# A decoder layer in float32: attention's values as split products, and its stages ordered head by head

## The chip, the cores and the metric

The kernel runs on one core of a Trainium2 chip. The metric is the time of one execution on the device in microseconds (us). Three runs of the kernel before took 1278.5 to 1279.03 us, median 1278.52. An execution that was profiled took 1277.71 us.

## The reference

One layer with a sequence of 1024 rows and a width of 1024, all in float32. A convolution branch and an attention branch are computed from the same normalised input and merged. Only attention matters here. It has 24 heads of 64 columns in three groups of eight, with a window and a stride for each group:

```python
DILATION_GROUPS = ((128, 1), (512, 4), (2048, 16))
...
scores = jnp.einsum('bdhnqe,bdhnke->bdhnqk', qb, kb) * (e ** -0.5)
scores = jnp.where(mask, scores, NEG_INF)
m = jnp.max(scores, axis=-1)
p = jnp.exp(scores - m[..., None])
den = jnp.sum(p, axis=-1)
o = jnp.einsum('bdhnqk,bdhnke->bdhnqe', p, vb) / den[..., None]
...
m_all = jnp.maximum(jnp.maximum(maxes[0], maxes[1]), maxes[2])
wts = [d_g * jnp.exp(m_g - m_all) for m_g, d_g in zip(maxes, dens)]
att = (wts[0]*outs[0] + wts[1]*outs[1] + wts[2]*outs[2]) / (wts[0] + wts[1] + wts[2])
y_att = (att * silu(z_att)) @ w_att_out
```

Queries are taken in blocks of 128. A block sees its own block of keys and, in the first two groups, also the one before it where there is one; the third group's blocks are packed so that each sees 128 keys.

## The kernel before, in words

Large products are made of three float32r products each: a float32 operand is written as a high part (ScalarE copies it into float32r) and a low part (VectorE or GpSimd subtracts the high part), and high x high, high x low and low x high are added up in PSUM. `split` (line 51) makes the parts, `mm3` (line 69) the products. One such product has a stationary operand of 128 x 128, loaded by its own LDWEIGHTS, and 512 moving columns.

The stretch that the change touches is a loop over slots (line 980 and on). In each slot TensorE first does one half of a projection half: twelve products of 512 columns (`pieces`), for the weights of k and q of the next heads and, at the end, for the gates. Behind it stands attention for one stage. There are twelve pairs of heads (j, g), four j by three groups g, and eight stages to a pair: a stage is two query blocks of one head, and before the change the two heads alternate from stage to stage. In slot s TensorE does, in this order, the scores of stage s, the turn (transposes) of stage s-2 and the values of stage s-3. Only TensorE's order is written out by hand; the other engines' and SyncE's orders are set by a scheduler that works on the recorded program.

- *Scores* (lines 843, 844). The stationary operand is q with its high part twice, or q_low (`ql`), the moving one k with both parts stacked over partitions; 128 or 256 keys. VectorE adds the mask and takes the row maximum (847), multiplies the two maxima by -1/8 (`nm`, 850), ScalarE takes the exponential and the row sum (852).
- *Turn* (860). Each 128 x 128 block of probabilities is transposed into PSUM `t` and copied into SBUF as `pt`, by VectorE in even stages (865) and by ScalarE in odd ones (863).
- *Values* (875). For each block of keys one float32 product of `pt` (stationary) with 64 columns of `vt`, into PSUM `o`; ScalarE copies `o` out after four stages (878).
- *Parts and moves.* A projection of k and q for one pair comes in two units (`part` 0 carries the rotated columns, lines 709 to 712, `part` 1 the others). `Parts` writes high and low parts into `kqp` (720, 721), a buffer of which there are two, and SyncE moves them into the stacked tiles: k2 and q2 of both heads when a part is made (`move_kq`), q_low of both heads and both parts later, in stage 4 of the pair before (`load_low`, with v's load). k2, q2 and ql have two tiles each, used in turn by pairs.
- *Combination.* After the third group of a j, `combine` reads the three groups' results back, weighs them by their maxima and row sums (897 to 922) and turns them (926); it is fed into later slots step by step through `beside`.

LEAD is the number of slots before the first stage, 13.

## Time and profile before

| | before |
|---|---|
| median of three runs | 1278.52 us |
| the profiled execution | 1277.71 us |
| its span, first to last instruction | 1275.9 us |
| TensorE busy | 1248.6 us (98%) |
| VectorE busy | 890.5 us (70%) |
| ScalarE busy | 476.8 us (37%) |
| GpSimd busy | 94.7 us (7%) |

Matmul groups of the page overlap in time, since a product begins before the one ahead of it has ended. What one product costs is therefore read from the distance between starts in the order of time, and how full the engine is from its idle time. Attention runs from about 676 to 1095 us of the span.

### The profile page before, as it was taken

What the parts mean: (1) busy time and instruction counts of PE and PEld (TensorE: products, weight loads), DVE (VectorE), ACT (ScalarE), POOL (GpSimd) and SP (SyncE); (2) the same over time, 40 slices, a digit from 0 to 9 for tenths busy, and PEclk for the clock granted to TensorE, in tenths of its full rate; (3) what the DMA queues carried; (4) which work ended last, traced back from release to release, by engine and by line L of the source; (5) the groups of instructions that cost most, each with busy time, mean ns of one, the idle gap of its engine ahead of it and who ended that gap; (6) DMA issues with size and microseconds to landing.
All of it is one profiled execution on the core that took longest, in us unless ns stands there. A gap on an engine that the chain in (4) does not pass through costs nothing.

```text
span 1275.9 us, 16604 instructions
## 1 busy us (share of the span) xinstructions
PE 1248.6 (98%) x6148; PEld 1050.6 (82%) x6148; DVE 890.5 (70%) x1576; ACT 476.8 (37%) x911; POOL 94.7 (7%) x78
## 2 busy tenths in 40 slices
PE   6999999999999999999999999999999989999997
PEld 4777888888888888888888888888888878888886
DVE  6777999999999986853345546766766563349544
ACT  4653212111222246720015545545444467534211
POOL 0000000000000000000042111111101012100000
PEclk9999999999999999999999999999999999999999
DMA  9522311211211112545666456576575566659221
GB/s 366 186 95 68 114 60 53 102 50 50 91 58 50 50 52 89 167 164 198 149 171 152 120 130 162 135 198 149 140 206 137 147 166 190 205 176 316 98 100 67
DMA packets 85526, 171.53 MB, mean 134 GB/s; under 512 B 11203, under 2 KB 41027, under 8 KB 85445
## 3 DMA queue, kind: packets, MB, share of 16 engines
q1 hardware_dynamic: 69024, 157.66, 41.9%
q10 hardware_dynamic: 16420, 12.80, 3.3%
q8 instruction: 49, 0.80, 0.3%
q14 instruction: 33, 0.26, 0.1%
HBM read 105.74 MB, written 33.23 MB: 109 GB/s over the span
## 4 chain that ended last, share of the span: by engine, by line
PE 91%; DVE 4%; DMA 2%; ACT 2%; issue 1%; SPq 0%; ACTq 0%; DVEq 0%
PE d L73 22%; PE d L75 22%; PE d L74 22%; PE o L875 4%; PE d L1070 2%; PE d L1069 2%; PE d L467 2%; PE d L466 2%; PE d L1071 2%; PE d L465 2%; PE t L860 2%; PE s L844 1%; PE s L843 1%; PE d L249 1%; PE d L247 1%; PE d L248 1%
## 5 line engine op out<-in xcount | busy, mean ns | idle before, releaser
L73 PE MATMUL d<-hh,whi 128*128 128x512 f32 x1072 | 427.5, 399 | 1.5 <-DVE gs L632 0.9
L74 PE MATMUL d<-hl,whi 128*128 128x512 f32 x1072 | 417.6, 390 | 1.9 <-DVE hl L347 1.9
L75 PE MATMUL d<-hh,wlo 128*128 128x512 f32 x1072 | 418.5, 390 | 0.0
L406 DVE SCALAR_TENSOR_TENSOR v<-u,cw,v 128x1024 f32<-128x1024 f32 x232 | 280.5, 1279 | 0.0
L75 PEld LDWEIGHTS d<-hh,wlo 128*128 128x128 f32 x1072 | 201.2, 188 | 43.9 <-POOL wlo L58 0.7
L74 PEld LDWEIGHTS d<-hl,whi 128*128 128x128 f32 x1072 | 201.7, 188 | 41.7 <-DVE hl L347 2.8
L73 PEld LDWEIGHTS d<-hh,whi 128*128 128x128 f32 x1072 | 201.6, 188 | 40.9 <-ACT whi L57 1.3
L57 ACT ACTIVATE whi<-wraw 128x512 fp32r<-128x512 f32 (+1 forms) x107 | 88.0, 834 | 269.6 <-PE d L74 236.1
L58 POOL TENSOR_TENSOR wlo<-wraw,whi 128x512 fp32r<-128x512 f32 (+1 forms) x56 | 84.8, 1529 | 658.0 <-ACT whi L57 556.2
L852 ACT ACTIVATE sb<-sb,nm 128x128 f32<-128x128 f32 (+1 forms) x192 | 85.0, 444 | 86.9 <-DVE nm L850 82.6
L847 DVE CUSTOM_DVE_ANT_0 sb<-s,mask 128x128 f32<-128x128 f32 (+1 forms) x192 | 59.7, 347 | 61.6 <-PE s L844 54.8
L875 PE MATMUL o<-vt,pt 128*128 128x64 f32 x560 | 73.5, 267 | 1.1 <-ACT pt L863 0.5
L875 PEld LDWEIGHTS o<-vt,pt 128*128 128x128 f32 x560 | 70.1, 192 | 2.1 <-DVE pt L865 1.3
L58 DVE TENSOR_TENSOR wlo<-wraw,whi 128x1024 fp32r<-128x1024 f32 (+1 forms) x51 | 57.9, 1137 | 15.6 <-ACT whi L57 15.0
L844 PE MATMUL s<-k,ql 128*128 128x128 f32 (+1 forms) x192 | 51.0, 279 | 3.2 <-DMA ql<-kqp 3.2
L465 PE MATMUL d<-vh,hh 128*128 128x512 f32 x128 | 49.8, 389 | 0.0
L466 PE MATMUL d<-vl,hh 128*128 128x512 f32 x128 | 49.8, 389 | 0.0
L467 PE MATMUL d<-vh,hl 128*128 128x512 f32 x128 | 49.8, 389 | 0.0
L73 PE MATMUL d<-uh,whi 128*128 128x512 f32 x128 | 49.8, 389 | 0.0
L74 PE MATMUL d<-ul,whi 128*128 128x512 f32 x128 | 49.8, 389 | 0.0
L75 PE MATMUL d<-uh,wlo 128*128 128x512 f32 x128 | 49.8, 389 | 0.0
L632 DVE TENSOR_TENSOR gs<-d,sgc 128x512 f32<-128x512 f32 x16 | 11.1, 691 | 54.9 <-PE d L75 48.8
(224 smaller groups left out, 1758.5 us busy)
## 6 DMA issues: line engine op xcount, KB each, us to landing
wraw<-in_w_t SPq DMA_DIRECT2D x67, 512.0 KB, 4.3
k<-kqp SPq DMA_DIRECT2D x96, 128.0 KB, 2.6
q<-kqp SPq DMA_DIRECT2D x96, 128.0 KB, 2.4
wa<-in_w_ada SPq DMA_DIRECT2D x16, 512.0 KB, 5.9
rd<-oscr SPq DMA_DIRECT2D x8, 792.0 KB, 5.1
ql<-kqp SPq DMA_DIRECT2D x48, 128.0 KB, 2.4
wraw<-in_w_v SPq DMA_DIRECT2D x11, 512.0 KB, 3.6
x<-in_xT SPq DMA_DIRECT2D x8, 512.0 KB, 10.2
```

Source lines behind the costliest of these rows:

```text
L57: nc.scalar.activation(hi, raw, AF.Copy)
L58: (lo_eng or nc.vector).tensor_sub(lo, raw, hi.bitcast(F32))
L73: nc.tensor.matmul(ps, lh, rh, start=start, stop=False)
L74: nc.tensor.matmul(ps, lh, rl, start=False, stop=False)
L75: nc.tensor.matmul(ps, ll, rh, start=False, stop=stop)
L406: nc.vector.scalar_tensor_tensor(d, u[:, k:k + S], cw[:, ct, k:k + 1], d, op0=mult, op1=add)
L465: nc.tensor.matmul(ps, hh[:, k, ts_], rh, start=k == 0, stop=False)
L466: nc.tensor.matmul(ps, hh[:, k, ts_], rl, start=False, stop=False)
L467: nc.tensor.matmul(ps, hl[:, k, ts_], rh, start=False, stop=k == KT - 1)
L844: nc.tensor.matmul(ps[:, c:c + w], self.ql[:, h, ts_], self.k2[:, h, ks], start=False, stop=True)
L852: nc.scalar.activation(sb[:, c:c + w], sb[:, c:c + w], AF.Exp, bias=nm[:, t - tp:t - tp + 1], scale=SCALE, accum_out=ov[:, t, h, 64:65])
L875: nc.tensor.matmul(self.po[:, t % 4, h], pt[:, c + i:c + i + P], self.vt[:, kb, r], start=i == 0, stop=i + P == w)
```

## The change

The values' product becomes float32r. The turned probabilities are split into `ph` and `pl`, each stage by ScalarE and VectorE together, and v is split too: a tile of one head holds for each block of 128 keys 64 columns of the high part and, side by side, 64 of the low part. Each block of keys then has two products, `ph` and `pl` as stationary operands with the same 128 moving columns, and all four products of parts are computed. PSUM `o` holds one head's results in two halves, which VectorE adds into `ov` after two stages (line 889).

To have tiles for this, k, q and q_low become tiles of one head, three each, used in turn by heads, and the eight stages of a pair go head by head: four stages of the first, four of the second. The moves go head by head as well: those of the first head when a part is made, those of the second one slot later or, for part 0, four slots before the pair begins, each with its q_low. v is loaded five slots ahead into a raw tile and split in steps. The mask pass multiplies by -1/8 and takes the minimum, so that its result serves as the exponential's bias and `nm` goes. LEAD becomes 11.

```diff
-    def pair_tile(n, name, dt=F32R):
-        return stk.tile([P, 2, S], dt, name=name, tag=f"s{n}")
+    def head_tile(tag, name):
+        return stk.tile([P, S], F32R, name=name, tag=tag)
...
     def move_kq(n, part, h):
+        i = turn_of(n, h)
         if not part:
-            k2[n], q2[n] = pair_tile(n % 2, "k2"), pair_tile(2 + n % 2, "q2")
-        move(k2[n], 0, n, part, 0, 0)
-        move(k2[n], 64, n, part, 0, 1)
-        move(q2[n], 0, n, part, 1, 0)
-        move(q2[n], 64, n, part, 1, 0)
+            k2[n, h], q2[n, h] = head_tile(f"k{i}", "k2"), head_tile(f"q{i}", "q2")
+        move(k2[n, h], 0, n, part, 0, 0, h)
+        move(k2[n, h], 64, n, part, 0, 1, h)
+        move(q2[n, h], 0, n, part, 1, 0, h)
+        move(q2[n, h], 64, n, part, 1, 0, h)
+        move(q_low[i], 0, n, part, 1, 1, h)
...
+        for h in range(2):
+            v = v2[n, h] = stk.tile([P, 8, P], F32R, name="vt", tag=f"v{turn_of(n, h)}")
+            src = raw[:, :, 64 * h:64 * h + 64]
+            nc.scalar.activation(v[:, :, 0:64], src, AF.Copy)
+            nc.vector.tensor_sub(v[:, :, 64:128], src, v[:, :, 0:64].bitcast(F32))
             yield
...
-            tp, h, o, out_ = st_ // 2 * 2, st_ % 2, 0, []
+            tp, h, o, out_ = st_ % 4 * 2, st_ // 4, 0, []
...
-                    out=sb[:, c:c + w], in0=ps[:, c:c + w], in1=mk, scale=1.0, scalar=-3e38, op0=add, op1=mx,
+                    out=sb[:, c:c + w], in0=ps[:, c:c + w], in1=mk, scale=-SCALE, scalar=3e38, op0=add, op1=ALU.min,
                     accum_out=ov[:, t, h, 65:66])
-            nc.vector.tensor_scalar(nm, ov[:, tp:tp + 2, h, 65], -SCALE, None, op0=mult)
             for t, c, w in spans:
-                nc.scalar.activation(sb[:, c:c + w], sb[:, c:c + w], AF.Exp, bias=nm[:, t - tp:t - tp + 1],
-                                     scale=SCALE, accum_out=ov[:, t, h, 64:65])
+                nc.scalar.activation(sb[:, c:c + w], sb[:, c:c + w], AF.Exp, bias=ov[:, t, h, 65:66],
+                                     scale=-1.0, accum_out=ov[:, t, h, 64:65])
...
-            pt = self.pt[st_] = ap_.tile([P, 512], F32, name="pt", tag="pt", bufs=2)
-            if st_ % 2:
-                nc.scalar.activation(pt[:, :o], ps[:, :o], AF.Copy)
-            else:
-                nc.vector.tensor_copy(pt[:, :o], ps[:, :o])
+            hi, lo = self.pt[st_] = [ap_.tile([P, 512], F32R, name=x, tag=x, bufs=2) for x in ("ph", "pl")]
+            split(hi[:, :o], lo[:, :o], ps[:, :o])
...
-                    nc.tensor.matmul(self.po[:, t % 4, h], pt[:, c + i:c + i + P], self.vt[:, kb, r],
-                                     start=i == 0, stop=i + P == w)
-            if st_ % 4 == 3:
-                nc.scalar.activation(self.ov[:, tp - 2:tp + 2, :, 0:64], self.po, AF.Copy)
+                    for x in range(2):
+                        nc.tensor.matmul(self.po[:, t % 4], parts[x][:, c + i:c + i + P], v[:, kb],
+                                         start=i == 0 and x == 0, stop=i + P == w and x == 1)
+            if st_ % 2:
+                nc.vector.tensor_reduce(self.ov[:, tp - 2:tp + 2, h, 0:64],
+                                        self.po.rearrange("p t (x c) -> p t c x", x=2),
+                                        axis=mybir.AxisListType.X, op=add)
...
-    LEAD, TURN, VAL = 13, 2, 3
+    LEAD, TURN, VAL = 11, 2, 3
...
+            for n, part in due:
+                move_kq(n, part, 0)
+                in_steps(moves(n, part, 1), [slot_ if n == 0 else slot_ + 1 if part else 8 * n - 4])
+            n = (slot_ + 5) // 8
+            if slot_ == v_slots(n)[0] and 0 <= n < len(order):
+                in_steps(load_v(n), v_slots(n))
```

After attention the freed tiles serve for the merged heads and the output weights under other names.

Three places show how instructions moved. The first is TensorE's order in one slot of the first group, from the last scores on (`s` scores, `t` turned probabilities, `o` results, `d` a projection); equal instructions that follow each other are merged into one row. Before:

```order
L843 MATMUL s<-k_6631,q_6632 128x256
L844 MATMUL s<-k_6631,ql 128x256
L860 MATMUL t<-ident,sb 128x128 x3
L875 MATMUL o<-vt,pt 128x64 x3
L73 MATMUL d<-hh,whi 128x512
L74 MATMUL d<-hl,whi 128x512
```

The same place afterwards:

```order
L857 MATMUL s<-k_6886,q_6887 128x256
L858 MATMUL s<-k_6886,ql 128x256
L873 MATMUL t<-ident,sb 128x128 x3
L886 MATMUL o<-vt,ph 128x128
L886 MATMUL o<-vt,pl 128x128
```

Each block of keys has two instructions of 128 columns in place of one of 64, each with its own stationary operand; such pairs follow each other for all blocks of the stage, and the projection comes behind them as before.

The second is VectorE's order where the last but one combination begins (`rd` the results read back, `ma`, `w`, `wd` the weights, `sb,ov` a mask pass). Before:

```order
L850 TENSOR_SCALAR nm<-ov 128x2
L897 TENSOR_TENSOR ma<-rd 128x8
L898 TENSOR_TENSOR ma<-ma,rd 128x8
L902 TENSOR_TENSOR w<-rd,ma 128x8 x3
L908 TENSOR_TENSOR wd<-w,rd 128x8 x3
L909 TENSOR_TENSOR wd<-wd 128x8
L910 TENSOR_TENSOR wd<-wd 128x8
L911 RECIPROCAL wd<-wd 128x8
L913 TENSOR_TENSOR w<-w,wd 128x8 x3
L917 TENSOR_TENSOR rd<-rd,w 128x4x2x64 x2
```

Afterwards, from the first low part of probabilities behind that combination's small operations and its three products on:

```order
L58 TENSOR_TENSOR pl<-t,ph 128x384
L721 TENSOR_TENSOR rot<-d,ctab 128x512
L889 TENSOR_REDUCE ov<-o 128x4x64
L722 TENSOR_TENSOR sh<-sh,stab 128x512
L933 TENSOR_TENSOR rd<-rd 128x4x2x64
L723 TENSOR_TENSOR rot<-rot,sh 128x512
L935 TENSOR_TENSOR pr<-rd 128x512
L861 ISA sb,ov<-s,mask 128x256
L861 ISA ov 128x1
L732 TENSOR_TENSOR kqp<-rot,kqp 128x32x16
```

Behind these rows stand one more mask pass and the next low part, `pl`. The rotation of the next heads (721 to 723, 732), the sum of halves (889) and the combination (933, 935) now lie between two low parts; the small operations, three products, a shuffle and two mask passes lie between the first of the two and the one ahead of it.

The third is SyncE's queue for the last pair of heads. Before:

```order
L785 DMA k_8055<-kqp 32x1024 x4
L785 DMA q_8056<-kqp 32x1024 x4
L929 DMA atscr_95<-at 128x512
L785 DMA ql<-kqp 32x1024 x4
L675 DMA vt<-vscr 64x8x128 x2
```

Afterwards, the end of the second head's moves for part 0, and then the moves for part 1 of both:

```order
L794 DMA q_8655<-kqp 32x1024 x2
L794 DMA ql<-kqp 32x1024
L794 DMA k_8481<-kqp 32x1024 x2
L794 DMA q_8482<-kqp 32x1024 x2
L794 DMA ql<-kqp 32x1024
L918 DMA at<-zascr_91 128x512
L794 DMA k_8654<-kqp 32x1024 x2
L794 DMA q_8655<-kqp 32x1024 x2
L794 DMA ql<-kqp 32x1024
```

q_low's moves stand behind those of the same head's k and q, one for each head and part, and v's load stands further ahead.

## Rows read from the trace of the kernel before

**Rows 1.** The page: busy us, share of span, instructions; out<-in xcount | busy, mean ns.

```profile
PE 1248.6 (98%) x6148; PEld 1050.6 (82%) x6148; DVE 890.5 (70%) x1576; ACT 476.8 (37%) x911; POOL 94.7 (7%) x78
...
L875 PEld LDWEIGHTS o<-vt,pt 128*128 128x128 f32 x560 | 70.1, 192 | 2.1 <-DVE pt L865 1.3
```

**Rows 2.** Sums over 676 to 1095 us: PE, PEld, DVE, ACT, POOL busy; granted clock.

```profile
676.00:1095.00 419.00, 414.12 (x2439) 362.26 (x2438) 247.85 (x808) 219.09 (x577) 65.49 (x44) 1.00 0.60 156
```

**Rows 3.** TensorE in order of time: start us, length us, operation, xcount.

```profile
801.03 0.60 PE L860 MATMUL t<-ident,sb 128*128 128x128 f32 x4
801.46 1.00 PE L875 MATMUL o<-vt,pt 128*128 128x64 f32 x8
...
802.59 0.39 PE L74 MATMUL d<-hl,whi 128*128 128x512 f32 x1
802.82 0.40 PE L75 MATMUL d<-hh,wlo 128*128 128x512 f32 x1
...
805.46 0.28 PE L844 MATMUL s<-k,ql 128*128 128x256 f32 x1
805.58 0.60 PE L860 MATMUL t<-ident,sb 128*128 128x128 f32 x4
```

**Rows 4.** TensorE in order of time, scores of 128 keys.

```profile
862.01 0.22 PE L843 MATMUL s<-k,q 128*128 128x128 f32 x1
862.07 0.28 PE L844 MATMUL s<-k,ql 128*128 128x128 f32 x1
862.18 0.27 PE L843 MATMUL s<-k,q 128*128 128x128 f32 x1
```

**Rows 5.** TensorE in order of time, instructions that waited [idle us <-releaser].

```profile
776.69 0.50 PE L73 MATMUL d<-hh,whi 128*128 128x512 f32 x1 [0.19 <-DVE rot L710]
...
845.42 0.30 PE L844 MATMUL s<-k,ql 128*128 128x128 f32 x1 [0.29 <-DMA ql<-kqp]
...
1028.47 0.88 PE L875 MATMUL o<-vt,pt 128*128 128x64 f32 x6 [0.53 <-DVE pt L865]
...
1052.50 0.30 PE L844 MATMUL s<-k,ql 128*128 128x128 f32 x1 [2.87 <-DMA ql<-kqp]
...
1062.52 0.88 PE L875 MATMUL o<-vt,pt 128*128 128x64 f32 x6 [0.54 <-ACT pt L863]
```

**Rows 6.** VectorE's groups, 640 to 1100 us, by shape: busy us, mean ns | idle.

```profile
L847 DVE CUSTOM_DVE_ANT_0 sb<-s,mask 128x256 f32<-128x256 f32 x88 | 35.1, 419 | 21.4 <-PE s L844 21.4
L850 DVE TENSOR_SCALAR nm<-ov 128x2 f32<-128x2 f32 x96 | 27.9, 291 | 1.6
...
L721 DVE TENSOR_TENSOR kqp<-rot,kqp 128x512 fp32r<-128x512 f32 x24 | 23.8, 993 | 24.5 <-ACT kqp L720 22.8 <-DMA vt<-vscr 1.6
...
L710 DVE TENSOR_TENSOR rot<-d,ctab 128x512 f32<-128x512 f32 x24 | 16.4, 684 | 0.4
...
L813 DVE TENSOR_TENSOR vt<-vt,row 128x512 f32<-128x512 f32 x8 | 5.3, 692 | 0.1
```

**Rows 7.** The same for all widths of VectorE's copies.

```profile
L865 DVE COPY pt<-t 128x384 f32<-128x384 f32 (+2 forms) x48 | 26.0, 541 | 0.0
```

**Rows 8.** ScalarE's groups, 640 to 1100 us.

```profile
L863 ACT ACTIVATE pt<-t 128x384 f32<-128x384 f32 (+2 forms) x48 | 22.8, 476 | 38.3 <-PE t L860 38.3
...
L878 ACT ACTIVATE ov<-o 128x512 f32<-128x512 f32 x24 | 14.2, 592 | 7.9 <-PE o L875 7.8
```

**Rows 9.** VectorE in order of time at the last but one combination.

```profile
1020.83 0.34 DVE L908 TENSOR_TENSOR wd<-w,rd 128x8 f32<-128x8 f32 x3 [0.53 <-ACT w L903]
...
1021.76 2.55 DVE L913 TENSOR_TENSOR w<-w,wd 128x8 f32<-128x8 f32 x3
1024.23 1.88 DVE L917 TENSOR_TENSOR rd<-rd,w 128x512 f32<-128x512 f32 x3
```

**Rows 10.** SyncE's queue in order of time: the last moves of q_low.

```profile
1047.29 3.99 SPq L785 DMA_DIRECT2D ql<-kqp  x4
```

**Rows 11.** SyncE's waits: us in total, times, longest us.

```profile
SPq L785 <- DMA ascr<-gs: 11.6, 2, 6.1
```

More of the change, by code (lines that the diff above doesn't have):

```diff
@@ L773, in pieces @@
                 yield lambda half=half, s=s, ps=ps: consume(half, s, ps)
-    LOW, UP = slice(0, 64), slice(64, 128)
-    q_low = [pair_tile(4 + i, "ql") for i in range(2)]
-    for ql in q_low:
-        nc.gpsimd.memset(ql[UP].bitcast(F32), 0.0)
     k2, q2, v2 = {}, {}, {}
-    def move(dst, row, n, part, i, which):
-        for h in range(2):
-            src = parts_of[n, part][64 * i + 32 * h:64 * i + 32 * h + 32, which]
-            nc.sync.dma_start(dst[row + 32 * part:row + 32 * part + 32, h].bitcast(F32), src.bitcast(F32))
@@ L787, in move_kq, with turn_of @@
-    def move_kq(n, part):
-        if not part:
-            k2[n], q2[n] = pair_tile(n % 2, "k2"), pair_tile(2 + n % 2, "q2")
-        move(k2[n], 0, n, part, 0, 0)
-        move(k2[n], 64, n, part, 0, 1)
-        move(q2[n], 0, n, part, 1, 0)
-        move(q2[n], 64, n, part, 1, 0)
-    late = []
-    def load_low(n):
-        for part in range(2):
-            move(q_low[n % 2], 0, n, part, 1, 1)
-        v2[n] = stk.tile([P, 8, P], F32, name="vt", tag="vt", bufs=2)
-        v_load(v2[n], order[n][1], order[n][0])
-        if order[n][1] == 0:
+    def turn_of(n, h):
+        return (2 * n + h) % 3
@@ new lines, in move, with move_kq @@
+    def move(dst, row, n, part, i, which, h):
+        src = parts_of[n, part][64 * i + 32 * h:64 * i + 32 * h + 32, which]
+        nc.sync.dma_start(dst[row + 32 * part:row + 32 * part + 32].bitcast(F32), src.bitcast(F32))
+    def move_kq(n, part, h):
+        i = turn_of(n, h)
+        if not part:
+            k2[n, h], q2[n, h] = head_tile(f"k{i}", "k2"), head_tile(f"q{i}", "q2")
[4 more added lines that the diff above has]
+        move(q_low[i], 0, n, part, 1, 1, h)
@@ L821, in __init__ @@
             self.j, self.g = order[n]
-            self.ql = q_low[n % 2]
-            self.k2, self.q2, self.vt = k2.pop(n), q2.pop(n), v2.pop(n)
+            self.n = n
+            self.ql = [q_low[turn_of(n, h)] for h in range(2)]
             self.ov = ap_.tile([P, 8, 2, 66], F32, name="ov", tag="ov", bufs=2)
@@ L948, in w_out @@
             hi, lo = (pool.tile([P, 1024], F32R, name=f"{x}{n}{kp}") for x in ("oh", "ol"))
-        elif kp < 2:
-            if not pairs:
-                pairs.update({i: pair_tile(4 + i, "oh") for i in range(2)})
-            hi, lo = pairs[0][:, kp], pairs[1][:, kp]
-        elif n:
-            both = pair_tile(0, "o13")
+        elif n == 0 and kp > 1:
+            both = parts_tile("oh")
             hi, lo = both[:, 0], both[:, 1]
         else:
-            hi, lo = (stk.tile([P, 1024], F32R, name=x, tag="vt", bufs=2) for x in ("oh", "ol"))
+            hi, lo = (head_tile(x, "oh") for x in {(0, 0): ("l2", "v0"), (0, 1): ("v1", "v2"), (1, 3): ("k0", "k1")}[n, kp])
         split(hi, lo, raw)
@@ L968, in layer, with in_steps, moves, v_slots @@
     beside, heads = {}, {}
+    def in_steps(it, slots):
+        for x in slots:
+            beside.setdefault(x, []).append(it)
+    def moves(n, part, h):
+        move_kq(n, part, h)
+        yield
+    def v_slots(n):
+        return [8 * n + x for x in (-5, -3, -2, 0, 1)]
     with tc.manual_schedule(engines={nc.tensor.engine}):
@@ L981, in layer @@
                     heads[n] = Attend(n)
-                if st_ == 4 and n + 1 < len(order):
-                    load_low(n + 1)
                 heads[n].scores(st_)
@@ L1000, in layer @@
                 next(c)
-            for c in late:
-                for x in (2, 2, 3):
-                    beside.setdefault(slot_ + x, []).append(c)
-            late[:] = []
             j = slot_ - stages - VAL
```

65 lines of the change are left out of this document (38 added, 27 removed).

## The prediction

> **What bounds the kernel now.** I read the page's busy times first: TensorE 98% of the span [rows 1]. A share near one can still hide waiting, so the second view is the sum over the attention stretch, 676 to 1095 us, the only one whose code changes: TensorE 414.12 of 419 us, VectorE 247.85 (59%), ScalarE 219.09 (52%), granted clock 1.00, the 2.4 GHz level [rows 2]. The reader should see that TensorE's own instructions set the length here. All its idle time in the stretch is some 5 us; no other saving can be larger unless TensorE's instructions themselves get cheaper.
>
> Third, the order of time on TensorE, for what one instruction costs. The groups of the page overlap, so I take the distance between starts. In a slot with four key blocks the eight records of the value product begin at 801.46, and the second wide product behind them at 802.59; one wide product is 0.23 us apart from the next (802.59 to 802.82). So the eight took 1.13 - 0.23 = 0.90 us, 0.1125 us each [rows 3]. They are float32: the code's loops make 280 products, but the page counts 560 weight loads [rows 1] (and as many records), two for each. A float32r product with 128 moving columns stands in the score products: 862.01, 862.07, 862.18: 0.06 behind the first of a burst, then 0.11 us [rows 4].
>
> Fourth, TensorE's waits of the stretch, of which there are few: 2.87 and 0.29 us for q_low's move, 0.53 for VectorE's copy of the turned probabilities, 0.54 for ScalarE's, and three times about 0.19 for the rotation that frees a projection bank (one shown) [rows 5]. Together 4.8 us.
>
> **The change part by part.**
>
> *Value products.* 280 float32 products of 64 columns go, 560 float32r products of 128 columns come. Before: 560 x 0.1125 = 63.0 us. After: 560 x 0.11 = 61.6 to 62.7 us (0.11 to 0.112, the score products' distance). Change on the path: 0 to -1.4 us; I take -0.4. The reason for equality is that records of 64 columns, of 128 columns and of two kinds of number all stand 0.11 us apart, and what they share is one weight load of 128 columns each; the number of weight loads stays 560. The ends: nothing in this trace has a float32r product of 128 columns behind another at less than 0.11 except the first of a burst (862.01 to 862.07, 0.06 us [rows 4]), whose load lay under a wide product; at that price the 560 would save 29 us. Upwards, the 256-column products stand 0.12 us apart (805.46 to the turn's 805.58 [rows 3]), +4 us.
>
> A page of the Trainium skill speaks for a gain here: "TensorE: Matmul & The Clock Gate", section "Back-to-back issue gap", gives about 81 ns for each product of 128 columns in a sustained stream with its weight loads. By that the 560 would take 45 us and the sum would fall by 18 us. The score products at 110 ns do not bear it out for these types.
>
> *VectorE.* Removed: 96 negated maxima, 27.9 us (mean 291 ns, some stretched), and 48 copies of turned probabilities, 26.0 us. Added: 96 low parts. They have the same widths as the copies, twice as many, and a product read from PSUM beside SBUF costs what a copy of the same width does (684 ns for 512 columns; the copies' mean is 541 over 256 to 512), so 52.0 us. 48 sums of the two halves of a result, 512 elements read: no such operation is in the trace; between 0.42 us (a mask pass over 256 columns) and 1.0 us (the strided low part of k and q), that is 20 to 48 us, and I take 0.68, the two-source pass over PSUM of the same width: 33 us. 24 low parts of v at 0.69 (the row addition of the same width): 16.6 us. Sum 52.0 + 33 + 16.6 - 27.9 - 26.0 = +48 us (+35 to +63) [rows 6, 7]. VectorE goes from 59% to about 71% of the stretch. This lies beside TensorE as long as the low part of the probabilities is ready one slot later.
>
> *ScalarE.* 48 more high parts, +22.8 us; 24 copies of results go, -14.2; 24 high parts of v come at about the same 0.59, +14.2 [rows 8]. 52% becomes 58%, hidden.
>
> *The added wait.* TensorE's value product of a stage now waits for ScalarE's copy and then VectorE's subtraction, where before it waited for one of them. A slot lasts 4.55 us (801.03 to 805.58 [rows 3]); the turn ends it, so 4.55 - 0.59 (ScalarE's copy of 512 columns [rows 8]) - 0.69 (subtraction) = 3.3 us of slack remain. Queued behind a late subtraction on VectorE are the next stage's mask passes, the rotation that frees a projection bank, and the sums. The tight place is the combination of three groups, which now stands in VectorE's order beside the rotation of the next heads. By that order, between two subtractions: 14 small operations (1.6 us at 0.34 for three), a wait of 0.53 for ScalarE's weights, three products 1.88, the shuffle taken at 0.69, two mask passes 0.84, the subtraction of 384 columns 0.54: 6.1 us; then eight operations of 512 columns at 0.69 and two passes 0.84: 6.4 us. 12.5 us in two slots of 4.55 leaves VectorE 3.4 us late against 3.3 of slack: 0.1 us of waiting. Stretched operations come on top; three small products at this place once took 2.55 instead of 0.34 us [rows 6, 7, 9]. So 0.1 to 2.4 us at each of three such places; I take 1.0, that is +3.0, less the 0.53 that stands there already: +2.5.
>
> *Moves.* The 240 transfers of k, q and q_low stay 240, but q_low's now go with the same part's k and q. Before, both parts' stood last in SyncE's queue; the last four were begun at 1047.29, after SyncE had waited up to 6.1 us for a store of gates, and TensorE waited for them until 1052.50 [rows 5, 10, 11]. Afterwards q_low's first part goes out four slots earlier, and the moves of the last heads stand in the queue ahead of the first store of gates, which ScalarE issues only after them. Both waits for q_low go: -3.2 us. What could be late next is the new wait of the second head's moves for the scores three heads earlier; they are issued one slot after those end and used eight slots later, so I cost it at 0; if SyncE is held by it for more than two slots (9 us), the overwriting of the parts' buffer waits. The float32r parts of v are made three slots ahead, 0 as well.
>
> *Earlier start and shape.* LEAD 13 to 11 moves no TensorE instruction out of the loop. The rotation meets the long slots instead of the short ones, which gives its bank release half a microsecond more: -0.3 of the 0.6. Two fewer slots of exponentials share ScalarE with the gates' sigmoids: no TensorE wait is charged to that, 0.
>
> Sum against the profiled execution's own 1277.71 us (span 1275.9 and 1.8 around it): -0.4 + 2.5 - 3.2 - 0.3 = -1.4, so 1276.3. That execution lies 0.8 us under the median 1278.52, so in medians 1277.1 us.
>
> **Rivals.**
>
> *The waits go and none comes (faster).* -0.4 - 4.8 = -5.2: 1273.3 us. For it: VectorE has 12 percentage points less than a full load even so, and it loses the negated maxima, which ScalarE waited for. Against: the combination overfills two slots by the count above.
>
> *VectorE is late (slower).* One mechanism: the low part of the probabilities, at the three combinations. It decides once VectorE is more than 3.3 us behind. With sums at 1.0 us and one stretched group each, a combination costs 0.1 + 2.2 + 4 x 0.31 = 3.5 us and the lateness lasts into the next rotation with as much again less the slack regained, say 3.5 to 7 us a place; -3.6 - 0.3 - 0.5 + 3 x 4 to 3 x 5 = +7.6 to 10.6, about 1287 us. For it: VectorE had a wait there already at less load, [rows 5]. Against: 71% mean load.
>
> *The values get cheaper (faster).* If float32r products stood as the first of a burst does, 0.06 us apart, the 560 would take 34 us instead of 63: 29 us less, 1249 us. For it: that one distance. Against: every other distance in [rows 3, 4]. By the Trainium skill's 81 ns ("TensorE: Matmul & The Clock Gate", "Back-to-back issue gap") it would be an estimated 1260.
>
> **How the numbers follow.** My forecast, a shift of 1 to 2 us: 0.40. Waits gone: 0.29. Values cheaper: 0.03. VectorE late: 0.28. What a measurement of this kernel can tell from no change is about 0.2%, 2.6 us: below 1276.0 is faster, above 1281.1 slower. The forecast's own range is 1275 to 1280; 0.04 of its 0.40 lies below that bound and 0.01 above. Of the waits that go, 0.25 of 0.29 is faster; of VectorE late, 0.26 of 0.28 is slower. Faster 0.32, same 0.41, slower 0.27. The range of eight in ten reaches to most of both neighbours: 1272.0 to 1285.5.
>
> **What would show it.** Right: 560 records of the value product still about 0.11 us apart, with 560 weight loads; TensorE's wait for q_low gone; new waits, if any, named "pl" and lying at the three combinations; VectorE near 295 us in the stretch. Wrong: value records at 0.06 to 0.08 (the values step); waits for "pl" spread over all slots, or for "k2" and "q2" (the slack and the moves); a sum of halves over 1 us (VectorE's step).

## The result, and the profile after

The changed kernel took 1282.91 us (median of 8 runs, 1281.95 to 1284.77) against 1278.93 for the kernel before (8 runs, 1276.84 to 1280.48): ratio 1.0032, 95% interval 1.0021 to 1.0043, slower by 0.32%. The forecast was 1277.1, a fall of 1.4 us; the medians rose by 4.0. The profiled execution took 1283.09 us and its span is 1281.3, 5.4 us more than before. That is 1.4 us more than the medians differ, mostly because the profiled execution of the kernel before (1277.71) lies 1.2 us under its median. What follows accounts for the two profiled executions.

The page after, groups as in [rows 1, 6 and 8] (out<-in xcount | busy, mean ns | idle), and behind it the sums over the stretch of [rows 2]:

```profile
PE 1250.6 (98%) x6148; PEld 1050.8 (82%) x6148; DVE 932.8 (73%) x1600; ACT 489.6 (38%) x957; POOL 91.8 (7%) x79
...
L58 DVE TENSOR_TENSOR pl<-t,ph 128x384 fp32r<-128x384 f32 (+2 forms) x96 | 52.2, 544 | 29.1 <-ACT ph L57 28.4
...
L57 ACT ACTIVATE ph<-t 128x384 fp32r<-128x384 f32 (+2 forms) x96 | 46.0, 480 | 58.8 <-PE t L873 56.5
L886 PEld LDWEIGHTS o<-vt,pl 128*128 128x128 f32 x280 | 53.7, 192 | 4.5 <-DVE pl L58 4.4
L886 PEld LDWEIGHTS o<-vt,ph 128*128 128x128 f32 x280 | 53.5, 191 | 2.9 <-ACT ph L57 2.8
```

```profile
676.00:1095.00 419.00, 412.34 (x2420) 359.97 (x2419) 284.91 (x830) 230.70 (x620) 60.59 (x43) 1.00 0.59 158
```

TensorE's weight loads for the values are 560 as before and its instruction count is the same. In the stretch VectorE carries 37 us more, ScalarE 12. TensorE's waits after (us in total, times, longest):

```profile
PE o L886 <- DVE pl L58: 2.6, 9, 0.6
PE s L857 <- DVE ov L861: 2.3, 1, 2.3
...
PE o L886 <- ACT ph L57: 1.2, 2, 0.9
PE d L73 <- ACT gs L740: 0.9, 1, 0.9
```

No wait for q_low or for the rotation's bank is left [rows 5]; four others have come. Where they stand is best seen in the distance from the first scores of a slot to those of the next, taken from TensorE's order of time. "Free" is the changed kernel with its order mended (a_best4 below), in whose stages TensorE waits nowhere: what the slots take without a wait. Slots that a wait made longer are bold in the column after, and in the column before in the last row alone.

| slots, us | before | after | free |
|---|---|---|---|
| 0 to 3 (start) | 3.19 3.19 3.57 4.23 | 3.19 **5.73** 3.71 4.32 | 3.19 3.22 3.57 4.35 |
| 32 to 35 (first combination) | 4.55 4.56 4.45 4.84 | **4.97** 4.52 **5.37** **5.03** | 4.57 4.52 4.43 4.19 |
| 80 to 83 (third combination) | 4.55 4.56 4.45 5.41 | **4.97** 4.52 **5.85** 4.61 | 4.57 4.52 4.43 4.19 |
| 88 to 94 (last pair) | **7.61** 4.17 **5.05** 3.83 3.84 3.83 3.84 | 4.59 **5.01** 4.07 **4.41** 3.81 **5.38** 3.81 | 4.15 4.15 4.07 3.86 3.81 3.86 3.81 |

Before and after, 0.4 us of slots 35, 83 and 88 are the transposes of a combination, which are work; in the free version they stand in other slots. From first to last scores the free version takes 397.7 us, and the kernel before without its waits 397.8 (b_ql below, its one slot with a wait counted as 4.57). After takes 408.7: 2.6 of waiting at the start, 5.4 at the three combinations (1.8 each), 2.9 in the last pair; another 1.05 stands behind the last stage. Before took 405.0: 3.5 for q_low, 1.2 for the rotation's bank, 1.4 at the combinations, 1.0 in the last pair. The difference of the waits, 12.0 - 7.1 = +4.9 us, is the 5.4 us between the spans but for 0.5 us. These waits are what the slots lost, which is more than the idle time in the list above: a product that waits does not overlap with the one ahead of it (below, 0.73 us between two starts for an idle time of 0.40, against 0.11 to 0.15 without a wait).

The start, VectorE in order of time (start us, length us):

```profile
671.26 0.75 DVE L720 STREAM_SHUFFLE sh<-d 128x512 f32<-128x512 f32 x1
672.04 1.59 DVE L722 TENSOR_TENSOR sh<-sh,stab 128x512 f32<-128x512 f32 x1
673.55 2.17 DVE L732 TENSOR_TENSOR kqp<-rot,kqp 128x512 fp32r<-128x512 f32 x1
675.76 0.69 DVE L721 TENSOR_TENSOR rot<-d,ctab 128x512 f32<-128x512 f32 x1
...
678.32 1.04 DVE L732 TENSOR_TENSOR kqp<-rot,kqp 128x512 fp32r<-128x512 f32 x1 [1.15 <-ACT kqp L731]
679.27 0.28 DVE L861 CUSTOM_DVE_ANT_0 sb<-s,mask 128x128 f32<-128x128 f32 x1
```

The scores of slot 0 were there at 671.3; their mask passes stand behind the whole second rotation of pair 1 and run at 679.3. The third scores need their bank and wait 2.35 us for it. Order is not all of it: two of these operations lie beside GpSimd's work and are stretched, L722 to 1.59 us from the usual 0.68 and the first L732 to 2.17, where no L732 without GpSimd beside it takes over 1.21 (see the last section). What the order would cost without that, no run tells.

A combination, VectorE, and TensorE's values of the same slot:

```profile
813.37 1.18 DVE L732 TENSOR_TENSOR kqp<-rot,kqp 128x512 fp32r<-128x512 f32 x1 [1.18 <-ACT kqp L731]
814.46 0.16 DVE L910 TENSOR_TENSOR ma<-rd 128x8 f32<-128x8 f32 x1
...
816.50 0.69 DVE L58 TENSOR_TENSOR pl<-t,ph 128x512 fp32r<-128x512 f32 x1
817.11 0.31 DVE L926 TENSOR_TENSOR w<-w,wd 128x8 f32<-128x8 f32 x3
817.34 1.89 DVE L930 TENSOR_TENSOR rd<-rd,w 128x512 f32<-128x512 f32 x3
```

```profile
816.52 0.19 PEld L886 LDWEIGHTS o<-vt,ph 128*128 128x128 f32 x1 [0.32 <-ACT ph L57]
816.52 0.33 PE L886 MATMUL o<-vt,ph 128*128 128x128 f32 x1
817.25 0.33 PE L886 MATMUL o<-vt,pl 128*128 128x128 f32 x1 [0.40 <-DVE pl L58]
817.41 0.28 PE L886 MATMUL o<-vt,ph 128*128 128x128 f32 x1
817.52 0.27 PE L886 MATMUL o<-vt,pl 128*128 128x128 f32 x1
817.63 0.28 PE L886 MATMUL o<-vt,ph 128*128 128x128 f32 x1
```

The combination follows a rotation at once, and `pl` comes 0.4 us late by the idle time; its product begins 0.73 us behind the one ahead of it. `ph` is late too: its weight load waits 0.32 us for ScalarE. Together they are nearly all of the 0.94 us that this slot loses. Behind the wait the products stand 0.11 us apart, as forecast.

In the kernel before, the combination at the same place begins 1.8 us behind the end of a rotation, with a low part and mask passes between, and slots 32 to 35 lose 0.3 us in all:

```profile
812.87 1.17 DVE L721 TENSOR_TENSOR kqp<-rot,kqp 128x512 fp32r<-128x512 f32 x1
...
815.82 0.17 DVE L897 TENSOR_TENSOR ma<-rd 128x8 f32<-128x8 f32 x1
```

So it is not new that the two are neighbours. It is new that every stage needs ScalarE and then VectorE.

The last pair, ScalarE:

```profile
1067.55 1.28 ACT L740 ACT_TABLE_LOAD   x1
1068.84 0.60 ACT L740 ACTIVATE gs<-d 128x512 f32<-128x512 f32 x1
1069.46 1.28 ACT L865 ACT_TABLE_LOAD   x1
1070.75 0.40 ACT L865 ACTIVATE sb<-sb,ov 128x128 f32<-128x128 f32 x1
...
1071.54 0.63 ACT L57 ACTIVATE ph<-t 128x256 fp32r<-128x256 f32 x2
```

Around one gate's sigmoid two tables are loaded, and `ph`, which every stage now needs from ScalarE, is 0.9 us late. (The Trainium skill, "ScalarE: Activation LUTs", section "What ACT_TABLE_LOAD costs", gives 2.66 us a switch with a drain; here the load begins 0.02 us behind the sigmoid and the next activation 1.29 us after it, so a switch costs its row.)

### The profile page after: what moved, and what is told of

Same layout as the page of the kernel before. It is cut to its first block, busy times and chain, and to the rows that moved or that the text cites. A ratio compares the mean times of both kernels' runs of the same rounds, so it can differ in the third digit from the quotient of the medians.

```text
span 1281.3 us, 16765 instructions
## 1 busy us (share of the span) xinstructions
PE 1250.6 (98%) x6148; PEld 1050.8 (82%) x6148; DVE 932.8 (73%) x1600; ACT 489.6 (38%) x957; POOL 91.8 (7%) x79
## 5 line engine op out<-in xcount | busy, mean ns | idle before, releaser
L865 ACT ACTIVATE sb<-sb,ov 128x128 f32<-128x128 f32 (+1 forms) x192 | 84.6, 442 | 45.2 <-DVE ov L861 44.8
L58 DVE TENSOR_TENSOR pl<-t,ph 128x384 fp32r<-128x384 f32 (+2 forms) x96 | 52.2, 544 | 29.1 <-ACT ph L57 28.4
L886 PE MATMUL o<-vt,ph 128*128 128x128 f32 x280 | 71.1, 286 | 1.4 <-ACT ph L57 1.2
L886 PE MATMUL o<-vt,pl 128*128 128x128 f32 x280 | 68.1, 277 | 2.9 <-DVE pl L58 2.6
L57 ACT ACTIVATE ph<-t 128x384 fp32r<-128x384 f32 (+2 forms) x96 | 46.0, 480 | 58.8 <-PE t L873 56.5
L886 PEld LDWEIGHTS o<-vt,pl 128*128 128x128 f32 x280 | 53.7, 192 | 4.5 <-DVE pl L58 4.4
L886 PEld LDWEIGHTS o<-vt,ph 128*128 128x128 f32 x280 | 53.5, 191 | 2.9 <-ACT ph L57 2.8
L1089 PE MATMUL d<-oh,hl 128*128 128x512 f32 (+1 forms) x136 | 51.2, 376 | 0.0
L1087 PE MATMUL d<-oh,hh 128*128 128x512 f32 (+1 forms) x136 | 51.2, 376 | 0.0
```

Source lines behind the costliest of these rows:

```text
L57: nc.scalar.activation(hi, raw, AF.Copy)
L58: (lo_eng or nc.vector).tensor_sub(lo, raw, hi.bitcast(F32))
L865: nc.scalar.activation(sb[:, c:c + w], sb[:, c:c + w], AF.Exp, bias=ov[:, t, h, 65:66], scale=-1.0, accum_out=ov[:, t, h, 64:65])
L886: nc.tensor.matmul(self.po[:, t % 4], parts[x][:, c + i:c + i + P], v[:, kb], start=i == 0 and x == 0, stop=i + P == w and x == 1)
L1087: nc.tensor.matmul(ps, hh[:, k, c], rh, start=k == 0, stop=False)
L1089: nc.tensor.matmul(ps, hl[:, k, c], rh, start=False, stop=k == KT - 1)
```

## The experiments

All against the kernel before on the same chip (median 1278.6 to 1278.9 there).

| run | us | ratio, 95% |
|---|---|---|
| b_lead11 | 1311.65 | 1.0257 (1.0233 to 1.0281) |
| a_lead12 | 1292.68 | 1.0103 (1.0087 to 1.0118) |
| a_poolcomb | 1285.31 | 1.0055 (1.0043 to 1.0068) |
| a_copygate | 1280.45 | 1.0011 (1.0002 to 1.0020) |
| a_start | 1281.45 | 1.0019 (1.0010 to 1.0027) |
| a_comb | 1277.71 | 0.9989 (0.9980 to 0.9998) |
| a_best, a_best3 | 1275.46, 1274.65 | 0.9973, 0.9971 (0.9962 to 0.9982) |
| a_best4, a_best5 | 1275.10, 1274.53 | 0.9973, 0.9967 (0.9957 to 0.9983) |
| a_best2 | 1277.17 | 0.9989 (0.9980 to 0.9998) |
| b_tanh | 1280.58 | 1.0015 (1.0006 to 1.0024) |
| b_ql | 1273.19 | 0.9960 (0.9946 to 0.9975) |
| b_ql2, b_ql2t | 1279.45, 1279.01 | 1.0009, 1.0006 (0.9997 to 1.0018) |
| a_nopl, a_nopl5 | 1279.23, 1264.10 | 1.0008 (0.9996 to 1.0020), 0.9887 (0.9869 to 0.9905) |

### LEAD by itself

```diff
-    LEAD, TURN, VAL = 13, 2, 3
+    LEAD, TURN, VAL = 11, 2, 3
-                if st_ == 4 and n + 1 < len(order):
+                if st_ == 5 and n + 1 < len(order):
```

> The kernel before with LEAD 11 instead of 13 and nothing else of the change, except that q_low and v are loaded in stage 5 of the pair before instead of stage 4, since the parts are made two slots later. Theory (the start): the first mask passes then stand on VectorE behind the rotation of the second pair, as in the changed kernel, and TensorE's third scores wait some 2.4 us for a bank of s; time +2.5 us on the kernel before, about 1281.4, plus up to 1 us where the rotation meets the combination, plus up to 1 us for q_low, issued one slot later. Rival (the new work): the late start of the mask passes needs the split of the probabilities and the order head by head; then LEAD alone shows no such wait, and the time stays at 1278.9 or falls by up to 1 us, since two slots fewer of exponentials share ScalarE with the gates' sigmoids.

```diff
-    LEAD, TURN, VAL = 11, 2, 3
+    LEAD, TURN, VAL = 12, 2, 3
```

> The changed kernel with LEAD 12 instead of 11. Theory (the start): the rotation of the second pair is one slot ahead of the first scores, the slot of 5.73 us at the start falls to about 3.2, time -2.5 us on the changed kernel, about 1280.4; at the combinations the rotation's second half comes one slot earlier too, so that these waits (1.75 us a place) may fall or rise by up to 1 us each; one slot more of exponentials among the gates' sigmoids, 0 to +1. Rival (new work alone): all waits come from VectorE's additional 48 us wherever the rotation stands; then the time stays within 0.8 us of the changed kernel's 1282.9.

In a_lead12 the start is as expected: slots 0 to 2 take 3.19, 3.22, 3.60. In b_lead11 the first slot takes 5.78 us instead of 3.19, which has the size of the theory but not its cause. TensorE waits there for q_low's move, and no wait for a bank of `s` follows (slots 1 and 2 take 3.19 and 3.68):

```profile
674.24 0.30 PE L844 MATMUL s<-k,ql 128*128 128x128 f32 x1 [2.38 <-DMA ql<-kqp]
```

So this run neither shows nor excludes that LEAD 11 alone delays the first mask passes. The times miss by far: in b_lead11 eleven of the twelve pairs have one slot that is 1 to 6.5 us too long. Its VectorE at one of the others, and TensorE:

```profile
819.32 1.57 DVE L711 TENSOR_TENSOR sh<-sh,stab 128x512 f32<-128x512 f32 x1
820.82 2.25 DVE L721 TENSOR_TENSOR kqp<-rot,kqp 128x512 fp32r<-128x512 f32 x1
...
826.73 0.68 DVE L865 COPY pt<-t 128x512 f32<-128x512 f32 x1
```

```profile
827.46 1.97 PE L875 MATMUL o<-vt,pt 128*128 128x64 f32 x8 [3.53 <-DVE pt L865]
```

The copy of the probabilities now stands behind two rotations. (Behind this wait the granted clock is 0.51 for 6 us, so the slot loses 6.5 us, not 3.5; see the last section.) In a_lead12 the third combination makes slots of 5.58, 5.55, 5.43 and 8.51 us out of 4.57, 4.52, 4.43 and 4.24. So most of what LEAD does to the time comes by the order in which the scheduler, given other phases, queues VectorE's work. Neither run isolates the start; the next ones do.

### The start alone, the combination alone

The second rotation of pair 1 is queued on VectorE behind the mask passes of slot 0:

```diff
-            if after:
+            if after and slot_ == 0:
+                with tc.issue_after(masked.ins):
+                    after()
+            elif after:
                 after()
```

> The changed kernel with one pair of VectorE's tasks exchanged: the second rotation of the second pair, which falls due in slot 0, is queued on VectorE behind the mask passes of slot 0; LEAD stays 11. Theory (order on VectorE at the start): the slot of 5.73 us falls to about 3.2, and nothing else moves, so -2.5 us on the changed kernel, about 1280.4. Rival (the amount of work on VectorE at the start, not its order): the wait only moves to the projection bank or to a later slot, and the time stays within 0.8 us of 1282.9.

1281.45, a gain of 1.5 us. Slot 1 fell from 5.73 to 3.22, but slot 3 rose from 4.32 to 5.62, with 0.56 us for `ph` and 0.27 for `pl` named there: half as expected, half the rival. (Queued behind slot 1's passes instead, in a_best4, slots 0 to 3 take 3.19 3.22 3.57 4.35.)

```diff
-    FIRST, SECOND = (2, 6, 6, 7, 7, 9), (8, 11, 11, 12, 12, 14)
+    STEPS = ((2, 8, 8, 9, 10, 12), (11, 18, 18, 20, 22, 24))
...
+            for c in pinned.pop(slot_, ()):
+                with tc.issue_after(pin.ins):
+                    next(c)
```

`pin` is the subtraction that makes `pl` in that slot.

> The changed kernel with the combination's steps, for the first three of four, tied on VectorE behind the low part of the probabilities of a slot in which no rotation runs (slots 2, 4 and 6 of a pair in place of 0, 1 and 3, and the second half in the next pair); the amount of VectorE's work is the same. Theory (combination and rotation in the same slots): the slots of 4.97, 5.37, 5.03 and 4.59 us fall to 4.6, 4.4, 4.2 and 4.2, apart from 0.45 us for each of the two groups of transposes, wherever they now stand: 1.2 to 1.75 us at each of three places, -3.5 to -5 us on the changed kernel, about 1278.5. Rival (VectorE's additional 48 us overfill it wherever the combination stands): the waits move with the combination, and the time stays within 1 us of 1282.9.

(The last combination keeps its slots, but its steps are tied behind `pl` as well.) 1277.71, 5.2 us less than the changed kernel, a little more than expected, with every slot of pairs 3 to 10 at its free length. VectorE at the same combination:

```profile
827.79 0.56 DVE L876 TENSOR_TENSOR pl<-t,ph 128x384 fp32r<-128x384 f32 x1
828.25 0.70 DVE L931 TENSOR_TENSOR rd<-rd,w 128x512 f32<-128x512 f32 x1
828.99 0.69 DVE L934 TENSOR_TENSOR rd<-rd 128x512 f32<-128x512 f32 x1
829.71 0.69 DVE L936 TENSOR_TENSOR pr<-rd 128x512 f32<-128x512 f32 x1
830.32 0.28 DVE L861 CUSTOM_DVE_ANT_0 sb<-s,mask 128x128 f32<-128x128 f32 x1
```

The same work fills the gap between `pl` and the next mask passes. So VectorE's load was not too much: what cost time was that two heavy tasks stood in the same slots.

Taking the combination off VectorE instead of moving it:

```diff
-            nc.vector.tensor_mul(o[g], o[g], w[:, g].unsqueeze(3).to_broadcast([P, 4, 2, 64]))
+            nc.gpsimd.tensor_mul(o[g], o[g], w[:, g].unsqueeze(3).to_broadcast([P, 4, 2, 64]))
```

and the two sums likewise.

> The changed kernel with the five passes of 512 columns of each half combination (three products with the weights, two sums) on GpSimd instead of VectorE, 30 passes of 0.69 us. Theory (VectorE late at the combination): the slots of 5.37 and 5.03 us there fall to 4.4 and 4.6 (the last holds the four transposes of the combination, 0.45 us, which stay), so 1 to 1.7 us of 1.75 go at each of three places: -3 to -5 us on the changed kernel, 1278 to 1280. Rival A (the rotation and ScalarE's copy set the lateness, not the combination): the slots stay as they are, 1282 to 1283. Rival B (GpSimd needs 1.3 us a pass, 6.5 us for five behind 2.5 us of weight splits): the combination's transposes wait on TensorE, 1 us or more at six places, 1286 or more.

1285.31, which none expected. The slots of 4.97 and 5.03 us did fall to 4.57 and 4.61, 2 us in all; 5.41 stayed. The loss lies behind the stages: the edit moved the fourth combination too, and from the last values to the first merged product it takes 55.3 us instead of 51.3, with 3.3 us of waiting for a gate's bank.

### ScalarE's tables

```diff
-            nc.scalar.activation(y, ps, AF.Sigmoid)
+            nc.scalar.activation(y, ps, AF.Copy)
```

> The changed kernel with a plain copy in place of the sigmoid of the attention gates, so that ScalarE loads no tables between sigmoids and exponentials; the sigmoid of these gates is left out. Theory (ScalarE in the tail): the waits for ph, pl and the gate's bank of the last pair (slots of 5.01, 4.41 and 5.38 us, and 1.05 us behind the last scores) go, -2.5 to -3 us on the changed kernel, about 1280. Rival: table loads lie beside TensorE and the waits there are VectorE's; then within 0.8 us of 1282.9.

1280.45, 2.5 us less, as expected; the last pair's slots are 4.59 4.15 4.87 3.86 3.81 3.86 3.81. This version leaves the sigmoid out. A hyperbolic tangent gives the same gates, with one added and the halves taken in later passes:

```diff
-            nc.scalar.activation(y, ps, AF.Sigmoid)
+            nc.scalar.activation(y, ps, AF.Tanh, scale=0.5)
```

> The changed kernel with the two edits of order just described and, in place of the gates' sigmoid, a hyperbolic tangent of half the argument, which ScalarE has in one table with the exponential (one is added and the product taken in the pass that took the product, and the factor one half goes into the combination's weights). Theory: the three terms add up, -2.5 at the start, -3.5 to -5 at the combinations, -2.5 in the last pair (as the plain copy in place of the sigmoid gave), so 1273 to 1275, under the kernel before by 0.3 to 0.45%. Rival: with one wait gone the next is late and half of it comes back, 1277 to 1279.

1275.46, with the edits of a_start and a_comb beside it: 7.5 of the 9.1 us that the three gave one by one.

> The kernel before with the same tangent in place of the sigmoid and nothing else. It tells whether that gain belongs to the change. Theory: before the change ScalarE's lateness in the last pair cost TensorE 0.5 to 1 us besides the 3.2 us for q_low, which waits on SyncE behind a store of gates; without table loads that store comes sooner too, so -0.5 to -3 us on the kernel before, 1276 to 1278.4. Rival: what ScalarE delays there lies beside TensorE, 1278.9.

1280.58, 1.7 us slower, which neither of the two expected. The order on the queues changed: q_low's wait in the last pair fell from 2.87 to 1.42 us, but a load of gate weights made ScalarE's copy 3.6 us late (slot 90: 9.64 us). So this run does not tell what the tables alone cost the kernel before.

### Is anything left of the change itself?

The rest of the versions ask what both kernels take without waits. First with LEAD 12 and other tied slots:

```diff
-    STEPS = ((2, 8, 8, 9, 10, 12), (11, 18, 18, 20, 22, 24))
+    STEPS = ((2, 7, 7, 9, 11, 13), (12, 15, 15, 17, 21, 23))
```

> As the last version with all edits of order, but with LEAD 12 in place of the exchanged pair of tasks at the start, the combination's steps tied to the slots that are free of rotations at that lead (slots 1, 3, 5 and 7 of a pair), and the split of the first merged heads tied on ScalarE and VectorE behind the last stage, so that it can't stand in front of exponentials while its load is under way. Theory (only the place of VectorE's work decides, not LEAD): the 10 us that LEAD 12 alone cost do not come back, the start is clean (no slot of 5.6 us), so 1.3 us less than the version with LEAD 11, and 0.5 to 1 us less in the last pair: 1273 to 1274. Rival (LEAD 12 is bad in itself, by q and k that come late or ScalarE in the last pair): 1280 or more.

1277.17: with LEAD 12 and another order most of the 10 us are gone, so that was order; but two slots of 5.7 us are left. With LEAD 11 again, the split of the first merged heads tied behind the last stage (a_best3), then the start mended too (a_best4), then that without the tie (a_best5):

```diff
-                    att_parts(j, s, raw[:, s])
+                    with tc.issue_after(pin.ins), tc.issue_after(pin_a.ins):
+                        att_parts(j, s, raw[:, s])
```

> The last version with all edits of order and LEAD 11, and the split of the first merged heads tied behind the last stage. Theory: the slot of 5.07 us in the last pair falls to 4.1, -1 us on that version, about 1274.5. Rival: the tied splits delay the merged product after attention, then as much or more is lost there, 1275.5 to 1277.

```diff
+            if slot_ == 1:
+                with tc.issue_after(masked.ins):
+                    kept()
...
+            if slot_ == 0:
+                kept = after
```

> The changed kernel with all edits of order, LEAD 11, and the second rotation of the second pair queued behind the mask passes of slot 1 in place of slot 0. Theory: the slot of 5.6 us at the start falls to 4.3, -1.3 us on the version before this one, about 1273.3; still no less than the kernel before with q_low moved, since the change removes nothing from TensorE. Rival: the change is worth something of its own once its waits are gone, and this kernel comes out under that one by 2 us or more.

> The last version without the tie of the merged heads' split behind the last stage: combination tied to slots without a rotation, the second pair's second rotation behind the mask passes of slot 1, tangent for sigmoid, LEAD 11. Theory: attention's stages keep no wait but the one slot of 5.1 us in the last pair (+1.0), and the 2.3 us behind the last stage with what the clock added go (-3.9), so -2.9 us on the last version, 1272.2: within 0.15% of the kernel before with q_low's moves earlier (1273.2), so that the change has no worth of its own that can be measured. Rival: under 1270, then it has.

1274.65, 1275.10 and 1274.53: none differs from a_best beyond its interval. In a_best4 no wait of TensorE is left in the stages, but a gate waits 2.3 us behind them; in a_best5 the gate waits 1.6 us and one stage 0.9. Part of what one place gives, another takes.

In the kernel before, q_low's moves one slot after the part's k and q:

```diff
-        for part in range(2):
-            move(q_low[n % 2], 0, n, part, 1, 1)
...
+                beside.setdefault(slot_ + 1, []).append(low(*x))
```

> The kernel before with q_low's moves issued one slot after the k and q of the same part instead of all in stage 4; nothing else of the change. It asks whether the gain on q_low needs the change. Theory: the 3.2 us of waiting for q_low go and nothing else moves, so 1275.7, the same as the changed kernel without its waits (1275.5), and the change itself is worth nothing beyond that. Rival: SyncE's queue, with the first store of gates in it, holds these moves as before, and the time stays at 1278.9.

1273.19, without the change the lowest median of the complete kernels. Its five executions fall into two groups, 1276.1 and 1276.5, and 1272.2 to 1273.2; the profiled one is the slowest and still waited once:

```profile
1049.29 0.48 PE L845 MATMUL s<-k,ql 128*128 128x128 f32 x1 [2.72 <-DMA ql<-kqp]
...
1053.53 0.63 PE L75 MATMUL d<-hh,wlo 128*128 128x512 f32 x1
1053.96 0.63 PE L73 MATMUL d<-hh,whi 128*128 128x512 f32 x1
```

Part 1's moves at once, to be rid of it (b_ql2t has the tangent beside it):

```diff
-                beside.setdefault(slot_ + 1, []).append(low(*x))
+                if x[1]:
+                    next(low(*x))
+                else:
+                    beside.setdefault(slot_ + 1, []).append(low(*x))
```

> The kernel before with q_low's moves issued with the k and q of the same part (part 1 at once, part 0 one slot later, since the tile is still read in that slot). Theory (the order of SyncE's queue alone makes the wait): the last moves no longer stand behind a store of gates, no wait for q_low is left, and what the last version lost there in its profiled run (2.7 us of waiting and 3.2 at a TensorE clock of one half behind it) goes in every run: 1270 to 1272, under the changed kernel without its waits (1274.7). Rival: the store of gates gets ahead of these moves again, 1273 or more.

> The same with the tangent in place of the gates' sigmoid. Theory: with q_low out of the way, the tables' share of the last pair's waits goes as in the changed kernel, -0.5 to -2 us on the version without the tangent, 1269 to 1271. Rival: as with the tangent alone in the kernel before, another order on ScalarE costs more than the tables did, +1.5 us or more.

1279.45 and 1279.01, both against the theory. No wait for q_low is left, but the gate weights now come late:

```profile
1043.72 0.50 PE L73 MATMUL d<-hh,whi 128*128 128x512 f32 x1 [3.44 <-ACT whi L57]
...
1046.15 0.79 PE L75 MATMUL d<-hh,wlo 128*128 128x512 f32 x1 [1.53 <-POOL wlo L58]
1046.75 0.63 PE L73 MATMUL d<-hh,whi 128*128 128x512 f32 x1
```

That slot takes 11.87 us. Mended, the changed kernel (a_best5, 1274.5) and the kernel before (b_ql, 1273.2) are the same within their intervals, and so are their stages without waits (397.7 and 397.8 us). The runs show no worth of the change by itself.

### The price of a value product

For the changed kernel and for a_best5, the products of `pl` are left out:

```diff
-                    for x in range(2):
+                    for x in range(1):
```

> The changed kernel without the products of the low part of the probabilities (that part is left out; it is still computed). 280 of 560 weight loads and products of the values go. Theory (a product of 128 columns costs its weight load, 0.112 us): -31.4 us and the waits for pl, about 1250 us, a gain that the change would have had by half the loads alone. Rival (by the 0.057 us that a product of 128 columns takes behind a wide one): -16 us, about 1267.

> The same without the products of the low part of the probabilities (left out, as before). Theory (a product of 128 columns costs 0.112 us with its weight load, and order decides the waits): with the combination away from the rotation most of the 280 x 0.112 = 31.4 us are gained this time, 1241 to 1248. Rival (ScalarE and VectorE bound the shorter slots wherever their work stands): again within 10 us of the kernel with these products, 1262 or more.

1279.23 and 1264.10: 4 and 10 us less than with these products, where the theory had 31. In undisturbed slots it holds: four products less make 4.55 us into 4.09, three 4.19 into 3.89, two 3.83 into 3.60, 0.10 to 0.12 us each. Most of the rest is eaten by waits for `ph`, 20.9 and 16.5 us by the profile, most of them where a rotation or a combination stands. That the shorter slots leave VectorE and ScalarE too little room there is the likely reason, but was not tested. Tying the combination alone did not free it.

## Why the prediction was wrong

**Right.** *Value products*: 0.112 us each after as before, 560 loads, and the two kernels' stages without waits lie within 0.1 us of each other. The 81 ns of the Trainium skill ("TensorE: Matmul & The Clock Gate", "Back-to-back issue gap") do not appear in any run here for these types. *VectorE*: `pl` 52.2 us (52.0 forecast), the sums of halves 32.7 us, 0.68 each, as taken; in all +37 us, 11 less than forecast. *Moves*: both waits for q_low are gone, 3.5 us (3.2 forecast). The bank's waits went too, 1.2 us where 0.3 was charged.

**Wrong: the step "Earlier start and shape".** LEAD indeed moves no TensorE instruction out of the loop. But the step charged 0 to ScalarE, and nothing at all to what the earlier start does to VectorE's order, and both failed. The second rotation of pair 1 now falls due in slot 0, ahead of the first mask passes on VectorE: +2.6 us in the trace. (LEAD 12 has no such wait, and a_start and a_best4 take it away by order alone, though a_start loses half of it again in slot 3.) And ScalarE's `ph`, needed in every stage instead of every other, stands behind two table loads for each gate: 2.9 us in the last pair and 1.05 behind it against 1.0 before, +3.0 (a_copygate gives 2.5 back). With that the word "hidden" of the ScalarE step failed in the last pair, though its high parts took 46.0 us, as forecast. These steps counted busy shares and shared slots, not what stands in front of what.

**Mis-sized: the added wait.** The places (three combinations) and most of the name (`pl`; in one slot of each place also `ph`) were right, the price was not: 5.4 us, 1.8 a place where 1.0 was taken, less 1.4 before (0.5 taken): +4.0 for +2.5. It lay within the bound of 0.1 to 2.4 a place. The count took 0.69 us for the rotation's strided low part, which took 1.18 in the row above, and it took only VectorE to be late. That two heavy tasks stand in the same slots is shown by a_comb, which keeps every operation and loses the whole term; VectorE's mean load, 68% of the stretch, is not the cause. Why the neighbourhood costs more than before is open: the low part in every stage, the other operations added and LEAD 11 changed together, and no run has the changed kernel with LEAD 13. So the rival "VectorE is late" had the place and, with 1282.9, the side, but its price of 4 to 5 us a place, and lateness as its only cause, were wrong. (That rival's opposite, "The waits go", was given 12 percentage points less than a full load for VectorE; at 71% it is 29.)

By the terms as measured: values 0, waits at the combinations +4.0, q_low -3.5, bank -1.2, start +2.6, ScalarE +3.0, outside the stages +0.5: +5.4, the difference of the spans. That 0.5 is 0.4 us less ahead of attention and 0.9 more from the merged product on; it was not tested. The result lies inside the range of eight in ten, 1272.0 to 1285.5, but only since that range reaches far to both sides: the forecast's own direction and two of its terms were wrong.

## What to carry to other kernels

Where one engine is full and the rest run from queues that a scheduler orders, a change of phase (a lead, a slot number) costs or gains more than the operations it adds: list, for each slot that has two periodic tasks, what stands ahead of the value that the full engine waits for. Before crediting a change with a wait that it removes, remove the wait alone in the old kernel. A wait that is removed can return at the next place in the queue, as in a_start and b_ql2, so it is the sum of all waits that counts, and the gains of single edits need not add up (here 9.1 us one by one, 7.5 together).

## What the runs showed of the hardware

*A wait costs more than its length when TensorE's clock falls behind it.* Sums by stretch: a_nopl after a wait of 5.44 us, b_ql after 2.72 us and further on (last columns: granted clock, DMA share, GB/s):

```profile
808.70:814.80 6.10, 6.08 (x17) 4.97 (x18) 1.93 (x6) 1.47 (x5) 0.00 (x0) 0.51 0.86 218
```

```profile
1049.30:1055.60 6.30, 6.30 (x23) 5.69 (x24) 1.88 (x7) 3.16 (x6) 0.52 (x1) 0.50 0.96 350
1056.00:1062.00 6.00, 6.00 (x40) 5.36 (x39) 1.00 (x8) 2.38 (x6) 1.46 (x1) 1.00 0.42 145
```

For some 6 us the clock is the lower of its two levels, 1.2 GHz, and wide products stand 0.43 us apart instead of 0.23, so 2.72 us of waiting made a slot of 4.57 into 10.47. The kernel before waited 2.87 us for q_low at the same place [rows 5] and its clock stayed at 1.00 behind it (slot of 7.61). In b_lead11 a wait of 3.53 us was followed by 6 us at 0.51, one of 2.15 us by 1.00. Why some and not others, these rows do not tell.

*VectorE beside GpSimd.* The rotation's pass over two SBUF operands (L722) takes 0.68 us in all 12 cases without GpSimd beside it and 1.19 on average, up to 1.59, in the 12 with it; the pass of the same width with one operand in PSUM (L721) takes 0.68 either way (10 and 14 cases). The long operation at the start, 672.04, lies on this one of GpSimd:

```profile
671.78 1.30 POOL L58 TENSOR_TENSOR wlo<-wraw,whi 128x512 fp32r<-128x512 f32 x1 [8.32 <-ACT whi L57]
```

The Trainium skill says so ("GPSIMD Engine Reference", "1. Specifications": contention with VectorE instructions that have two SBUF inputs), and the trace agrees. The prediction's stretched operations fit it: in the kernel before, one small product (L913) takes 0.16 us in its 12 cases without GpSimd beside it and 0.90 on average in 6 with it, and the three that took 2.55 us together, from 1021.76 on [rows 9], lie beside this one of GpSimd:

```profile
1021.82 2.39 POOL L58 TENSOR_TENSOR wlo<-wraw,whi 128x1024 fp32r<-128x1024 f32 x1 [30.73 <-ACT whi L57]
```
